# Mixing stage of a hybrid diffusion step: four instead of six output tiles summed during attention, three summed in the end of the stage

## The chip, the core and the metric

The kernel runs on one core of a Trainium2 chip. The metric is device time in microseconds (us) of one execution. The engines are TensorE (PE: matmuls; PEld: its weight loads), VectorE (DVE), ScalarE (ACT), GpSimd (POOL) and SyncE (SP, which issues most DMAs). Each engine works through its own instructions in order; semaphores hold an instruction until what it reads is there.

## The reference

One inference step of a backbone with two layers, 1024 channels, 128 context tokens and 512 latent tokens. Cut to what matters here:

```python
def layer(x, cond, p, lam_init, ropes, ctx):
    h = modulate(rmsnorm(x, p['norm_ffn1']), sh1, sc1)
    x = x + 0.5 * g1 * swiglu(h, p['w_ffn1_in'], p['w_ffn1_out'])
    h = modulate(rmsnorm(x, p['norm_mix']), sh2, sc2)
    y, kv = token_mix(h, p, lam_init, ropes, ctx)
    x = x + g2 * y
    h = modulate(rmsnorm(x, p['norm_ffn2']), sh3, sc3)
    x = x + 0.5 * g3 * swiglu(h, p['w_ffn2_in'], p['w_ffn2_out'])
    return x, kv

def token_mix(h, p, lam_init, ropes, ctx):
    # h @ w_mix_in, split among four head groups of 256 channels each
    ...
    y = jnp.concatenate([y_pool, y_conv, y_gqa, y_diff], axis=-1) @ p['w_mix_out']
    return y, kv_out
```

`y` has 1024 channels: pooling gives the first quarter, a gated convolution the second, grouped-query attention the third, differential attention (with a norm of each head) the last. The change concerns the product with `w_mix_out`.

## The kernel before

Channels lie on the 128 partitions, so x and y are 8 tiles of 128 channels by 640 tokens. All is fp32 by pairs: a number is a high part (`hi`, made by ACT, L174) and a low part (`lo`, made by DVE or POOL, L175), and a product is three matmuls: high by high, high by low, low by high. The tokens go in two halves of 320 columns. One output tile d of the mixing product is thus 8 blocks of y by 3 by 2, 48 matmuls: 36 for y blocks 0 to 5 (`mix_sum`, with 768 columns of weights, `mix_w`) and 12 for blocks 6 and 7 (the "ends"). Blocks 6 and 7 come from differential attention; block 7 is ready last of all, after its head norm (`diff_norm`: head squares on `sel`, a row spread on ACT, transposes on `ident`, a split).

`mix` weaves two generators: `main()` runs the attention (scores, softmax on ACT and DVE, value products), `fill()` gives TensorE other work to do in its waits: projections, the convolution, and at the end the sums of output tiles NO to NO+NE-1, each in two F buffers of PSUM, added to x by three DVE updates (`x_update`, L529). Which comes when is set by two lists of weights, `wm` and `wf`. Tile 0 is opened after that in an S buffer, and gets its 36 matmuls while the last head norm runs.

The end of the stage begins with `mix_ends`, four weight pieces of 512 columns that hold the rows for y blocks 6 and 7 of all tiles (two tiles to a piece). Then a loop goes over the tiles in the ORDER 0, 4, 1, 5, 2, 6, 3, 7. It adds the ends, updates x, and calls `nx.tile(d)`, which prepares the next norm and FFN: squares (ACT L328, summed up on POOL L330), scaling (ACT L434) and, from tile 4 on, sums on DVE (L451 to L457) with splits (L196, L197). The norm's statistics product on `ones` comes once the last tile's square is in the sum. Before the change tile 7 is the one tile whose 36 matmuls come in this loop; its weights are requested when the loop reaches its fifth tile (WLATE = 4).

Weights come through 9 raw buffers, 4 `hi` and 4 `lo` buffers (tags shared by all weights); `mix_w` takes two pieces (512 and 256 columns), with the low part on POOL. PSUM has two S, two F and two H buffers. A scheduler places each instruction on its engine in the order it finds best, not simply as the code is written. In names, S, F and H are PSUM buffers, hi and lo weight pieces, u activation tiles, t scratch, raw weights as loaded, and wa weights of the modulation.

Of the kernel before, what the change touches and what calls it, by code (L numbers as in the profile page):

```python
# [17 lines left out]
WG = 1.7  # L18
LAG = 0.1
LASTN = 384  # L20
NO, NE = 1, 6
WARM = 6
POOLD = ()
SHO = range(8)
SPREAD = 3
RATES = (0.6, 0.42, 0.6)
WLATE = 4
P1A, P0B, P1B = 1, 2, 2
D = 1024
KT = 8  # L30
# [12 lines left out]
ORDER = (0, 4, 1, 5, 2, 6, 3, 7)  # L43
# [39 lines left out]
def hybrid_step(ctx: ExitStack, tc: tile.TileContext, x_in, cc_in, cb_in, w_ada0, w_ada, pv_in, lam_in, w_fin, w_fout, w_min, w_mout,  # L83
# [37 lines left out]
    def PS():  # L121
        return psS.tile([128, 2, 512], F32, tag="S", name=nm("S"))
# [11 lines left out]
    def mm(out, lhsT, rhs, start, stop):  # L134
        PE.matmul(out, lhsT, rhs, start=start, stop=stop)  # L135
# [14 lines left out]
    def raw_tile():  # L150
        return wp.tile([128, 512], F32, tag="raw", name=nm("raw"), bufs=RAWB)
# [31 lines left out]
    def load_w(src, eng=None):  # L183
        return Weights(load_raw(src), eng)
# [312 lines left out]
    def mm3(ps, cuts, w, acts, ks=range(KT), start=True, stop=True):  # L497

        for i, k in enumerate(ks):
            w0, w1 = w.at(k)  # L500
            ah, al = acts[k]
            for p, (w_, a) in enumerate(((w0, ah), (w0, al), (w1, ah))):
                for h in range(2):
                    c0, c1 = cuts[h]
                    mm(ps[h][:, :c1 - c0], w_, a[:, c0:c1],
                       start and i == 0 and p == 0, stop and i == len(ks) - 1 and p == 2)
# [17 lines left out]
    def x_update(d, ps, gate):  # L524

        g = gate[d // 4]
        for c, h, a, b in ((0, 0, 0, NC), (1, 0, NC, HN), (1, 1, 0, HN)):
            xs = x[d][:, h * HN + a:h * HN + b]
            V.scalar_tensor_tensor(out=xs, in0=ps[h][:, a:b], scalar=g[:, d % 4, c:c + 1], in1=xs,  # L529
                                   op0=ALU.mult, op1=ALU.add)  # L530
# [227 lines left out]
    def mix(l, norm, nxt, cache):  # L758
# [524 lines left out]
        def mix_w(d):  # L1283
            return load_w(w_mout[l, d, :, :768], G)

        def mix_sum(w, ps, d, start, stop):

            mm3(ps, CN, w, y, range(6), start, stop)

        def mix_ends():  # L1290

            r = []
            for d0 in (0, 4):
                raws = []
                for d in (d0, d0 + 2):
                    raws.append(raw_tile())
                    nc.sync.dma_start(raws[-1].rearrange("p (d n) -> p d n", d=2), w_mout[l, d:d + 2, :, 768:].rearrange("d p n -> p d n"))
                r.append(Weights(raws))
            return r
# [14 lines left out]
        def drain(*gens):  # L1314
            for g_ in gens:
                next(g_, None)
# [63 lines left out]
            drain(dn)  # L1380
        drain(dn, dn, dn)
        ends = mix_ends()
        for i, d in enumerate(ORDER):
            if d in opened:
                ps = opened[d]
            else:
                p = PS()
                ps = [p[:, 0], p[:, 1]]
            if i == WLATE and NO + NE < KT:
                wl = mix_w(NO + NE)  # L1390
            if d >= NO + NE:
                mix_sum(wl, ps, d, True, False)
            w, k = ends[d // 4], 2 * (d % 4)
            for q in range(2):
                w0, w1 = w.at(k + q)
                ah, al = y[6 + q]
                for p_, (w_, a) in enumerate(((w0, ah), (w0, al), (w1, ah))):
                    for h in range(2):
                        c0, c1 = CN[h]
                        mm(ps[h][:, :HN], w_, a[:, c0:c1], NO <= d < NO + NE and q == 0 and p_ == 0, q == 1 and p_ == 2)  # L1400
            x_update(d, ps, gate)
            nx.tile(d)
# [56 lines left out]
    cache = load_cache(0)  # L1459
    lambdas()  # L1460
    nx = mix(0, nx, lambda: FastNorm(0, 2), cache)
    cache = load_cache(1)
    rows = silu_rows()
# [4 lines left out]
    nx = ffn(1, 0, nx, lambda: Norm(1, 1), pump, RATES[2])  # L1468
    pump.step(1000)
    nx = mix(1, nx, lambda: FastNorm(1, 2), cache)  # L1470
    ffn(1, 2, nx, lambda: None, pump, 0.0)

# [111 lines left out]
```

## Time and profile before

| | us |
|---|---|
| median of 3 runs | 2451.6 (2450.91 to 2452.83) |
| the profiled execution | 2455.93 |
| its span | 2453.9 |
| PE busy in it | 2348.2 |
| DVE busy in it | 2072.6 |

The mean granted clock of TensorE is 0.979 of full speed in it. The span runs from the first instruction to the last; some 2 us of the execution lie around it. A timeline row gives a run of like instructions on one engine: its start, its length, what it is, how many there are, and in brackets how long the engine stood idle before and what released it.

### The profile page before, as it was taken

The page shows a single profiled execution, that of the slowest core. Times are in us where ns is not written, and L with a number is a line of the kernel's source. Part 1 is how long each engine was busy: PE and PEld are TensorE (multiplying, and loading weights), DVE is VectorE, ACT ScalarE, POOL GpSimd, SP SyncE. Part 2 cuts the span into 40 slices and gives each one's busy share as a digit, 9 for nine tenths or more (in the row PEclk, how much of TensorE's full clock was granted, in tenths as well). Part 3 has the DMA queues.
Part 4 walks back from the last instruction along what each step waited for, and adds up shares of the span by engine and source line. Part 5 has one row for each costly group of instructions (what it writes and reads, how often), then busy time and mean ns, then how long its engine had stood idle before and what let it go on. Part 6 is the DMA issues. An engine that isn't in the chain of part 4 may idle for free. (4 is left out here: it accounts for less than half of the span.)

```text
span 2453.9 us, 42559 instructions
## 1 busy us (share of the span) xinstructions
PE 2348.2 (96%) x15497; PEld 2286.1 (93%) x15497; DVE 2072.6 (84%) x3927; ACT 1249.9 (51%) x2498; POOL 377.3 (15%) x424
## 2 busy tenths in 40 slices
PE   7899999999998999999989999999999989999998
PEld 4899999998987999999979999999998979999997
DVE  5999999867878899999989997777687687867876
ACT  3635443557665635434565434445676564434434
POOL 3100000134323101000030100003422330000002
PEclk8999999999999999999989999999999999999999
DMA  7455554423323355555516554323232112223223
GB/s 268 124 181 155 163 165 149 115 89 125 123 80 114 81 182 154 167 156 163 154 61 163 150 163 113 101 76 106 85 141 92 57 40 86 79 83 93 83 71 97
DMA packets 156545, 297.43 MB, mean 121 GB/s; under 512 B 16176, under 2 KB 47536, under 8 KB 156336
## 3 DMA queue, kind: packets, MB, share of 16 engines
q1 hardware_dynamic: 142464, 278.01, 35.4%
q0 software_dynamic: 13872, 16.71, 4.5%
q8 instruction: 122, 2.00, 0.3%
q14 instruction: 87, 0.71, 0.1%
HBM read 263.00 MB, written 14.94 MB: 113 GB/s over the span
## 5 line engine op out<-in xcount | busy, mean ns | idle before, releaser
L174 ACT ACTIVATE hi<-raw 128x512 fp32r<-128x512 f32 (+2 forms) x954 | 574.4, 605 | 879.3 <-PE S L135 385.5
L175 DVE TENSOR_TENSOR lo<-raw,hi 128x512 fp32r<-128x512 f32 (+1 forms) x874 | 571.1, 659 | 109.8 <-ACT hi L174 104.6
L515 PE MATMUL F<-u,hi 128*128 128x322 f32 x2752 | 627.2, 315 | 1.4 <-DVE t L653 0.6
L135 PE MATMUL S<-u,hi 128*128 128x320 f32 (+3 forms) x2144 | 485.9, 317 | 42.1 <-DVE x L529 12.9
L515 PEld LDWEIGHTS F<-u,hi 128*128 128x128 f32 x2752 | 465.0, 190 | 7.2 <-DVE t L653 1.3
L515 PE MATMUL F<-u,lo 128*128 128x322 f32 x1376 | 427.4, 311 | 0.7 <-DVE lo L175 0.7
L135 PE MATMUL S<-u,lo 128*128 128x320 f32 (+3 forms) x1776 | 420.8, 313 | 3.3 <-DVE lo L175 2.5
L135 PEld LDWEIGHTS S<-u,hi 128*128 128x128 f32 x2144 | 361.6, 193 | 54.2 <-issue 16.7
L282 DVE SCALAR_TENSOR_TENSOR wa<-wa,sc 128x1024 bf16<-128x1024 f32 (+1 forms) x264 | 324.3, 1235 | 12.6 <-DMA wa<-in_w_ada_dram 9.0
L135 PE MATMUL S<-e,hi 128*128 128x320 f32 (+2 forms) x1408 | 329.6, 311 | 2.4 <-DVE e L197 1.9
L515 PE MATMUL S<-u,hi 128*128 128x322 f32 x1376 | 313.3, 314 | 12.0 <-DVE t L590 11.0
L135 PEld LDWEIGHTS S<-u,lo 128*128 128x128 f32 x1776 | 306.1, 192 | 4.5 <-DVE lo L175 3.4
L515 PEld LDWEIGHTS F<-u,lo 128*128 128x128 f32 x1376 | 263.9, 192 | 1.0 <-DVE lo L175 1.0
L627 DVE TENSOR_TENSOR raw<-raw,raw 128x512 f32<-128x512 f32 x344 | 238.6, 694 | 8.0 <-DMA raw<-in_w_fin_dram 3.6
L515 PEld LDWEIGHTS S<-u,hi 128*128 128x128 f32 x1376 | 233.0, 190 | 13.0 <-issue 11.2
L135 PEld LDWEIGHTS S<-e,hi 128*128 128x128 f32 x1408 | 237.5, 189 | 5.0 <-DVE e L197 4.8
L135 PE MATMUL F<-u,hi 128*128 128x320 f32 (+1 forms) x1056 | 239.8, 319 | 1.5 <-DVE x L529 0.8
L515 PE MATMUL S<-u,lo 128*128 128x322 f32 x688 | 214.6, 312 | 1.5 <-DVE lo L175 1.5
L572 POOL DMA_DIRECT2D e<-t x51 | 61.5, 1206 | 1003.7 <-DVE t L641 371.7
L540 DVE SCALAR_TENSOR_TENSOR x<-S,gate,x 128x128 f32<-128x128 f32 (+1 forms) x304 | 152.5, 544 | 46.6 <-PE S L135 45.4
L135 PEld LDWEIGHTS F<-u,hi 128*128 128x128 f32 x1056 | 179.0, 193 | 3.9 <-DVE x L529 0.9
L515 PE MATMUL H<-u,hi 128*128 128x322 f32 x688 | 156.3, 313 | 3.0 <-ACT hi L174 3.0
(232 smaller groups left out, 3195.4 us busy)
## 6 DMA issues: line engine op xcount, KB each, us to landing
raw<-in_w_fin_dram SPq DMA_DIRECT2D x352, 256.0 KB
wa<-in_w_ada_dram SPq DMA_DIRECT2D x132, 512.0 KB
raw<-in_w_fout_dram SPq DMA_DIRECT2D x168, 256.0 KB
raw<-in_w_min_dram SPq DMA_DIRECT2D x72, 256.0 KB
e<-t POOLq DMA_DIRECT2D x51, 320.0 KB, 5.3
u<-in_w_ada_dram SPq DMA_DIRECT2D x24, 256.0 KB
KS<-kd SPq DMA_DIRECT2D x16, 384.0 KB
raw<-in_w_mout_dram SPq DMA_DIRECT2D x24, 256.0 KB
```

Source lines behind the costliest of these rows:

```text
L135: PE.matmul(out, lhsT, rhs, start=start, stop=stop)
L174: S.activation(hi[:, :n], src, AF.Copy)
L175: (eng or V).tensor_tensor(out=lo[:, :n], in0=src, in1=hi[:, :n], op=ALU.subtract)
L282: V.scalar_tensor_tensor(out=o, in0=raw, scalar=1.0, in1=rows[i], op0=ALU.mult, op1=ALU.mult, accum_out=m[0][:, b, i:i + 1])
L515: PE.matmul(ps, w_, a, start=start and k == 0 and p == 0, stop=k == 3 and p == 2, skip_group_check=True)
L540: V.scalar_tensor_tensor(out=x[d][:, a:b], in0=w[:, a:b], scalar=g[:, d % 4, c:c + 1], in1=x[d][:, a:b], op0=ALU.mult, op1=ALU.add)
L572: G.dma_start(lo[:, :N].bitcast(F32).rearrange("p (h n) -> p h n", h=2), a, accum_op=ALU.add)
L627: V.tensor_tensor(out=o, in0=a, in1=b, op=ALU.add)
```

## The change

Tiles 1 to 4, not 1 to 6, are summed in `fill()`; the list `wf` is shorter by two entries, so the other fillers spread over attention anew. Tiles 5, 6 and 7 get all their matmuls in the loop at the end. Each one's weights are requested one tile ahead in ORDER, after the sum of the tile before: tile 5's with tile 1, tile 6's with tile 2, tile 7's with tile 3.

```diff
-NO, NE = 1, 6
+NO, NE = 1, 4
-WLATE = 4
...
         ends = mix_ends()
+        late = {}
         for i, d in enumerate(ORDER):
             if d in opened:
                 ps = opened[d]
             else:
                 p = PS()
                 ps = [p[:, 0], p[:, 1]]
-            if i == WLATE and NO + NE < KT:
-                wl = mix_w(NO + NE)
             if d >= NO + NE:
-                mix_sum(wl, ps, d, True, False)
+                mix_sum(late.pop(d), ps, d, True, False)
+            for n in ORDER[i + 1:i + 2]:
+                if n >= NO + NE:
+                    late[n] = mix_w(n)
```

Lines of the changed kernel are one lower (L134 for L135, and so on). Names get new numbers.

PE, layer 0, around the last head norm, before: the head squares (`sel`) follow 18 matmuls after the last value products; F_8662 and F_8715 are filler tiles, S_8823 is tile 0.

```order
L135 MATMUL F_8663<-u_8180,hi_8672 128x320
L135 MATMUL F_8662<-u_8179,lo_8673 128x320
L135 MATMUL F_8663<-u_8179,lo_8673 128x320
L135 MATMUL H_8872<-sel_97,t_8821 128x2 x5
L135 MATMUL F_8715<-u_7477,hi_8721 128x320
...
L135 MATMUL S_8823<-u_8180,hi_8832 128x320 x2
L135 MATMUL S_8823<-u_8179,lo_8833 128x320 x2
L944 MATMUL H_8885<-ident_96,t_8883 128x128 x4
L944 MATMUL H_8891<-ident_96,t_8883 128x128
```

The same place after, where S_8717 is tile 0 and S_8844 tile 4:

```order
L134 MATMUL S_8717<-u_8310,lo_8727 128x320 x2
L134 MATMUL H_8766<-sel_97,t_8715 128x2 x5
L134 MATMUL S_8717<-u_8161,hi_8796 128x320 x2
L134 MATMUL S_8717<-u_8162,hi_8796 128x320 x2
L134 MATMUL S_8717<-u_8161,lo_8797 128x320 x2
L134 MATMUL S_8844<-u_8161,hi_8808 128x320 x2
L134 MATMUL S_8844<-u_8162,hi_8808 128x320 x2
L134 MATMUL S_8844<-u_8161,lo_8809 128x320
L943 MATMUL H_8779<-ident_96,t_8777 128x128 x4
L943 MATMUL H_8785<-ident_96,t_8777 128x128
```

Where 108 matmuls lay between `sel` and the transposes (`ident`), 11 do now; the 108 lie ahead of `sel`, after the last value products. Ahead of those, 54 fewer stand in each layer.

PE, layer 0, tile 5 in the end loop, after; S_8901 is tile 1, S_8937 tile 5, S_9024 tile 2. Before, tile 5 had only 12 matmuls there.

```order
L134 MATMUL S_8901<-u_8788,lo_8797 128x320 x2
L134 MATMUL S_8937<-u_7553,hi_8906 128x320 x2
...
L134 MATMUL S_8937<-u_8401,lo_8907 128x320 x2
L134 MATMUL S_9024<-u_8161,hi_8800 128x320 x2
L134 MATMUL S_9024<-u_8162,hi_8800 128x320
L134 MATMUL S_8937<-u_7763,hi_8910 128x320 x2
```

Tile 5's first piece (hi_8906) serves 24 matmuls, its second (hi_8910) 12, and three of tile 2's come between them.

ACT, layer 0, the same place, after; u are splits of tiles 0 and 4 for the next FFN, x_82 is tile 1.

```order
L195 ACTIVATE u_8879<-t_8863 128x322
L173 ACTIVATE hi_8906<-raw_8902 128x512
L195 ACTIVATE u_8884<-t_8875 128x322
L195 ACTIVATE u_8887<-t_8874 128x322
L195 ACTIVATE u_8891<-t_8874 128x322
L327 ACTIVATE t_8929<-x_82 128x640
L433 ACTIVATE t_8932<-x_82,scl_8834 128x128
L173 ACTIVATE hi_8910<-raw_8904 128x256
```

Tile 5's two pieces stand between the splits of the next FFN; before, the one late tile's two pieces stood next to each other.

## Rows read from the trace of the kernel before

**Rows 1.** Page, part 1: busy us, share of the span, instructions.

```profile
PE 2348.2 (96%) x15497; PEld 2286.1 (93%) x15497; DVE 2072.6 (84%) x3927; ACT 1249.9 (51%) x2498; POOL 377.3 (15%) x424
```

**Rows 2.** Windows: us, busy time (count) by engine, PEclk, DMA share, GB/s.

```profile
560.00:747.00 187.00, 178.92 (x1227) 171.21 (x1226) 146.96 (x312) 126.45 (x294) 59.62 (x66) 0.98 0.33 111
773.00:805.00 32.00, 23.04 (x119) 22.13 (x119) 29.46 (x62) 21.64 (x53) 14.34 (x13) 0.79 0.12 40
1757.00:1944.00 187.00, 178.75 (x1225) 170.24 (x1225) 147.53 (x311) 128.29 (x293) 59.91 (x70) 0.98 0.30 101
1968.00:1997.00 29.00, 19.92 (x120) 18.99 (x121) 26.44 (x57) 21.59 (x53) 13.65 (x12) 0.94 0.06 19
```

**Rows 3.** Timeline of PE, layer 0: start, us, engine, line, operation, idle before.

```profile
746.08 0.76 PE L135 MATMUL H<-p,u 128*128 128x256 f32 x5
...
749.32 1.17 PE L135 MATMUL H<-sel,t 128*128 128x2 f32 x10
...
768.11 0.71 PE L944 MATMUL H<-ident,t 128*128 128x128 f32 x5
...
775.16 0.82 PE L135 MATMUL S<-u,hi 128*128 128x320 f32 x4 [0.92 <-DVE x L529]
...
794.69 1.40 PE L135 MATMUL S<-u,hi 128*128 128x320 f32 x4 [2.73 <-ACT t L434]
...
810.95 2.17 PE L135 MATMUL H<-ones,t 128*128 128x1 f32 x10 [2.29 <-POOL t L330]
```

**Rows 4.** Timeline of PE, layer 1.

```profile
1943.71 0.76 PE L135 MATMUL H<-p,u 128*128 128x256 f32 x5
...
1963.95 0.71 PE L944 MATMUL H<-ident,t 128*128 128x128 f32 x5
...
1983.27 1.27 PE L135 MATMUL S<-u,hi 128*128 128x320 f32 x4
1984.34 0.74 PE L135 MATMUL S<-u,lo 128*128 128x320 f32 x2
...
1995.65 0.74 PE L135 MATMUL S<-u,hi 128*128 128x320 f32 x4
1996.24 0.45 PE L135 MATMUL S<-u,lo 128*128 128x320 f32 x2
...
2001.65 1.67 PE L135 MATMUL H<-ones,t 128*128 128x1 f32 x10 [0.72 <-POOL t L330]
```

**Rows 5.** Timeline of DVE, layer 0.

```profile
771.94 0.81 DVE L197 TENSOR_TENSOR u<-u,u 128x640 fp32r<-128x640 f32 x1
...
773.89 2.16 DVE L529 SCALAR_TENSOR_TENSOR x<-S,mod,x 128x128 f32<-128x128 f32 x6
775.98 1.21 DVE L282 SCALAR_TENSOR_TENSOR wa<-wa,sc 128x1024 f32<-128x1024 f32 x1
```

**Rows 6.** Timeline of DVE, layer 1.

```profile
1966.98 0.83 DVE L197 TENSOR_TENSOR u<-u,u 128x640 fp32r<-128x640 f32 x1 [0.80 <-ACT u L196]
...
1975.16 2.52 DVE L197 TENSOR_TENSOR u<-t,u 128x322 fp32r<-128x322 f32 x2
...
1978.67 2.10 DVE L197 TENSOR_TENSOR u<-t,u 128x322 fp32r<-128x322 f32 x5
```

**Rows 7.** Timeline of ACT, layer 0.

```profile
752.78 0.74 ACT L936 ACTIVATE t<-s 128x640 f32<-128x640 f32 x1 [0.46 <-POOL s L1253]
...
779.24 0.92 ACT L174 ACTIVATE hi<-raw 128x512 fp32r<-128x512 f32 x2
```

**Rows 8.** Groups by line and shape, POOL: busy, mean ns, idle before, releasers.

```profile
L175 POOL TENSOR_TENSOR lo<-raw,hi 128x512 fp32r<-128x512 f32 x64 | 86.4, 1355 | 230.4 <-ACT hi L174 224.9 <-PE S L135 4.9 <-DVE t L789 0.3
...
L175 POOL TENSOR_TENSOR lo<-raw,hi 128x256 fp32r<-128x256 f32 x16 | 13.7, 853 | 5.1 <-ACT hi L174 4.8 <-PE S L135 0.2
```

**Rows 9.** Timeline of POOL, both layers.

```profile
777.59 1.81 POOL L330 TENSOR_TENSOR t<-t,t 128x640 f32<-128x640 f32 x1 [18.41 <-ACT t L328]
...
1974.79 2.54 POOL L175 TENSOR_TENSOR lo<-raw,hi 128x512 fp32r<-128x512 f32 x2 [0.76 <-ACT hi L174]
```

## The prediction

> **What bounds the kernel now.** I read the page's busy shares first. TensorE's matmuls (PE) are busy 96% of the span and VectorE (DVE) 84% [rows 1]. The change leaves every matmul in the program and only moves some, so it can pay only where PE stands still. I therefore cut the mixing stage of each layer by the table of windows [rows 2] and then read the timelines at the cuts. The reader is to see two places of opposite kind. During attention PE is busy 178.9 of 187 us at a clock of 0.98 while DVE is busy 147: softmax work has nearly enough matmuls under it. At the end of the stage PE is busy only 23 of 32 us in layer 0 at a clock of 0.79, and DVE 29.5 of 32; in layer 1 it is 19.9 and 26.4 of 29 us. There DVE is what the end waits for, and PE has room. The change carries matmuls from the first place to the second.
>
> Three marks per layer divide the time. P is the end of the last value products (128x256): 746.84 and 1944.47 [rows 3, 4]. T is the end of the split of y block 7, from which the last two y blocks can be used: 772.75 and 1967.81 [rows 5, 6]. S is the start of the statistics product of the next norm (on `ones`), which needs the last tile's sum: 810.95 and 2001.65. Before, P to T is 25.9 and 23.3 us, T to S is 38.2 and 33.8.
>
> **Attention, up to P.** In the new PE order 54 matmuls of 320 columns fewer stand ahead of P in each layer. At the full clock (2.4 GHz) one takes (1996.24 - 1995.65)/4 = 0.147 us [rows 4]: 7.9 us. What they covered, softmax's waits, does not go with them. Now 8.1 of 187 us are idle; with about 4% fewer filler matmuls I add an estimated 1.5 us. Bounds: 0 (the cover was spare) and 7.9 (each was cover). I take the low side, since the remaining filler still fills 96% of the window. Term: -6.4 us per layer.
>
> **From P to T.** Before, 18 matmuls come before the head-square products (on `sel`) and 108 between these and the transposes; after, 108 and 11. So PE no longer covers the chain from the squares over DVE, POOL and the ACT spread to the transposes. That chain takes 753.52 - 749.32 = 4.2 us in layer 0 [rows 3, 7], and 11 matmuls are 1.6 of it. From the transposes to T it is 4.6 and 3.9 us, as before [rows 3 to 6]. After: 108 x 0.147 = 15.9, plus 4.2, plus 4.6 or 3.9, is 24.7 and 24.0. Term: -1.2 in layer 0, +0.6 in layer 1.
>
> **From T to S.** Here 61 matmuls more wait: most of tiles 5, 6 and 7. Step by step from T, with layer 0's durations:
> PE restarts when the first update has freed an S buffer, at +2.4 (775.16) [rows 3]. Tile 1's 12 matmuls: +4.2. Tile 5's first weight piece needs a buffer which tile 1's weights hold until then, and on ACT it stands behind the splits of tile 4; ACT reached the weight piece at this place at 779.24, which is +6.5, and needs 0.46 [rows 7]: +7.0. POOL forms the low half in 1.36 [rows 8] and with the hand-overs I set +8.5. Four of the 24 matmuls run meanwhile; 20 are left, 2.9 us at the full clock. At the low level (1.2 GHz) one takes (1984.34 - 1983.27)/4 = 0.267 [rows 4], so 5.3: +11.4 or +13.8. The second piece finds no other free buffer than the first one's: 0.46, then 0.85 on POOL [rows 8] and 0.2 of hand-overs: +12.9 or +15.3. Another 20 matmuls (8 of the piece, 12 of the ends): +15.8 or +18.2. The three updates are half of 2.16 [rows 5], so tile 6 starts at +17.0 or +19.4. From here weights are ready, their buffers being free during the tile before: 48 matmuls of tile 6 take 7.1, 12 of tile 3 1.8, 48 of tile 7 7.1: +33.0 or +35.4. Then the update 1.1, the ACT square (as wide as the spread of 0.74 [rows 7]) and the POOL sum 1.8 [rows 9]: S at +36.6 or +39.0. Against 38.2 that is -1.6 to +0.8, against 33.8 it is +2.8 to +5.2; the middles are -0.4 and +4.0.
>
> Two weight pairs more per layer now have their low halves formed by POOL while DVE is the busy engine. In layer 1 a pair ran on POOL at 1974.79 for 2.54 [rows 9], and two DVE splits that began at 1975.16 took 2.52, where five took 2.10 shortly after [rows 6]: 1.26 each instead of 0.42. The rows alone bound the loss by the time of two pairs, 0 to 5.1 us per layer (2 x 2.54); DVE stands on the path of the end only in the updates, so I take about a quarter, +1.1. Term with it: +0.7 in layer 0, +5.1 in layer 1. The Trainium skill (SBUF — State Buffer, Who interferes with whom) says that a DVE instruction with two SBUF inputs contends with a GpSimd instruction that reads SBUF, and that whichever is first keeps the shared ports while the other stands still; the two splits above agree with it. Taken at its word for both pairs, and with DVE the pace of the end throughout, it would add 2 x 4.0 us to the sum, 2452.0 on the median.
>
> The waiting instructions hold others. On ACT the splits and scalings of tiles 4 and 1 stand around the late pieces; on POOL a square sum stands behind tile 5's low half; on DVE weight preparation for the next FFN (raw buffers) stands ahead of tile 5's update, and in layer 0 eight instead of three products of 1.21 us on `wa` [rows 5]: 6.1 us, hidden only while PE is the slower. I cost the requests themselves at nothing: the queue carries the same bytes and DMA is busy 0.12 and 0.06 in the two ends [rows 2]. If a request came late, tile 5 would wait for it.
>
> **Sum.** Layer 0: -6.4 - 1.2 + 0.7 = -6.9. Layer 1: -6.4 + 0.6 + 5.1 = -0.7. Together -7.6 us, or 2455.9 to 2448.3 of the profiled execution. That execution is 4.3 us above the median, 2451.6; on the median the same difference gives 2444.0.
>
> **Rivals.**
> *The low clock slows the late sums (slower).* In layer 0's end the granted clock is 0.79; after an idle of 2.73 us four matmuls take 1.40 where four at the full clock take 0.74 [rows 2 to 4]. Now PE waits several times in a row there (before the transposes, after T, for tile 5's two pieces), and 108 matmuls of late sums follow. If all run at 0.267 instead of 0.147 it costs 13.0 us per layer; 2.4 are in the middle above, so +10.6 per layer and +21 in both: 2465. The sum's gain is used up by 63 such matmuls beyond the 20 per layer already counted. Against it: layer 1's end has 0.94 now, and PE would be busier there than it is now. On gaps of this sort the Trainium skill (TensorE: Matmul & The Clock Gate, HAM oscillation) warns that they make the array run slow again for work that follows; by it the time is this rival's.
> *DVE still bounds the end.* With DVE at 29.5 of 32 us, the late sums may simply fill PE's gaps, and T to S stays as it is: -6.4 - 1.2 and -6.4 + 0.6, together -13.4, or 2438.2. Against it: tile 5's two pieces follow each other on a path that has no slack.
> *Attention isn't paced by PE.* If softmax's chain sets the pace, the 54 matmuls bring nothing up to P: -7.6 + 12.8 = +5.2, or 2456.8. Against it: PE is busy 96% there and at the full clock.
> *Part of it.* Half the attention term only (+6.4), or two POOL pairs that hold DVE for their whole 5.1 us in each layer (+8.0): 2450 to 2452. For it: the splits at 1975.16 [rows 6, 9]; against it: DVE has other idle gaps to lose first, 2.5 us in each end [rows 2].
>
> **How the numbers follow.** About 0.2%, 4.9 us, is what a measurement of this kernel can tell: faster is below 2446.7, slower above 2456.5. I give the sum 0.45 (0.38 faster, 0.07 within), DVE-bound end 0.13 (faster), partial 0.20 (0.17 within, 0.03 slower), low clock 0.12 (slower), attention not paced 0.10 (half within, half slower). Faster 0.51, same 0.29, slower 0.20. The sum's own range is 2439 to 2449, from both clock levels and part of the port loss; with the others on either side I set 2436 to 2457.
>
> **What would show it.** P comes 6 to 8 us earlier after the start of attention in both layers. The `sel` products follow some 100 matmuls after P, and PE then idles about 2.5 us before the transposes; T is 24 to 25 us after P. PE waits for an ACT weight piece and a POOL low half before tile 5, twice; T to S is 37 to 40 us in both layers. I am wrong if P does not move, if T to S passes 45 us, or if it stays at 38 and 34 or less.

## The result and the profile after

The changed kernel is slower: 2488.68 us median (2488.06 to 2490.18) against 2452.22 us for the kernel before beside it, ratio 1.0143 with a 95% interval of 1.0131 to 1.0155. The forecast was 2444.0 with a range of 2436 to 2457; it had the sign wrong.

The profiled execution after has a span of 2486.0 us, 32.1 more than before. The three marks of the prediction divide it, with the first softmax exponential of each attention as a fourth (in layer 0 the mark lies 0.7 us ahead of it, in every run alike; columns: layer 0, layer 1; us):

| stretch | before | after | forecast of the change | measured |
|---|---|---|---|---|
| first exponential to P | 185.7, 183.2 | 193.2, 187.3 | -6.4, -6.4 | +7.6, +4.1 |
| P to T | 25.9, 23.3 | 24.9, 24.2 | -1.2, +0.6 | -1.0, +0.8 |
| T to S | 38.2, 33.8 | 50.8, 44.0 | +0.7, +5.1 | +12.6, +10.1 |

These add up to +34.2; the stretches outside give back 2.1. Windows of the changed kernel, the columns as in [rows 2]; the first and third run from 16 us before the first exponential to P, the second and fourth from T to S:

```profile
545.00:754.30 209.30, 188.06 (x1252) 178.11 (x1251) 162.21 (x330) 131.75 (x307) 67.17 (x76) 0.95 0.31 103
...
779.20:830.00 50.80, 38.35 (x213) 35.50 (x212) 48.71 (x85) 28.95 (x66) 24.44 (x19) 0.89 0.25 78
1761.70:1965.20 203.50, 182.33 (x1238) 172.92 (x1237) 156.31 (x327) 130.81 (x303) 64.97 (x73) 0.97 0.28 96
...
1989.40:2033.30 43.90, 35.81 (x212) 33.44 (x210) 34.50 (x66) 28.30 (x66) 20.74 (x19) 0.93 0.10 31
```

In attention PE is idle 21.2 of 209.3 us where 10.4 of 201.7 were idle before, and 21.2 of 203.5 where it was 10.6 of 199.2: with less to do it waits longer. In the end of layer 0 DVE is busy 48.7 of 50.8 us, for the kernel before 29.5 of 32 [rows 2], or 34.2 of the whole 38.2. The matmuls that came into the end filled little of PE's idle time there: it is idle 12.4 us of T to S where it was 11.5, in layer 1 8.1 where it was 10.2.

The timeline of PE in layer 0, which answers to [rows 3]:

```profile
752.99 1.34 PE L134 MATMUL H<-p,u 128*128 128x256 f32 x10
...
770.07 1.17 PE L134 MATMUL H<-sel,t 128*128 128x2 f32 x10
...
775.66 0.76 PE L943 MATMUL H<-ident,t 128*128 128x128 f32 x5 [2.69 <-ACT t L935]
...
782.04 1.41 PE L134 MATMUL S<-u,hi 128*128 128x320 f32 x4 [0.25 <-DVE x L528]
...
786.78 1.30 PE L134 MATMUL S<-u,hi 128*128 128x320 f32 x4 [2.05 <-ACT hi L173]
...
795.61 0.56 PE L134 MATMUL S<-u,lo 128*128 128x320 f32 x2 [1.91 <-POOL lo L174]
...
801.36 0.82 PE L134 MATMUL S<-u,hi 128*128 128x320 f32 x4 [1.22 <-DVE x L528]
...
814.41 1.40 PE L134 MATMUL S<-u,hi 128*128 128x320 f32 x4 [4.01 <-DVE x L528]
...
830.04 1.28 PE L134 MATMUL H<-ones,t 128*128 128x1 f32 x10 [2.30 <-POOL t L329]
```

From P (754.33) on, the `sel` products, the 2.7 us of uncovered chain and T (779.24) lie as the prediction has them; P itself is 7.5 us later than before, where 6.4 us earlier was forecast. From T the steps are: tile 5 starts at +7.5, its second low half is there at +16.4, tile 6 starts at +22.1, tile 7 at +35.2, S at +50.8. The last two rows with DVE as releaser, PE's waits of 1.22 and 4.01 us, are where the time goes. DVE's own timeline at T, at these places and at the last update, and POOL's below it:

```profile
778.42 0.82 DVE L196 TENSOR_TENSOR u<-u,u 128x640 fp32r<-128x640 f32 x1
...
797.84 2.31 DVE L281 SCALAR_TENSOR_TENSOR wa<-wa,sc 128x1024 bf16<-128x1024 f32 x1
...
800.09 2.17 DVE L528 SCALAR_TENSOR_TENSOR x<-S,mod,x 128x128 f32<-128x128 f32 x6
...
805.86 2.31 DVE L281 SCALAR_TENSOR_TENSOR wa<-wa,sc 128x1024 bf16<-128x1024 f32 x1
...
813.14 1.12 DVE L528 SCALAR_TENSOR_TENSOR x<-S,mod,x 128x128 f32<-128x128 f32 x3
...
825.46 1.12 DVE L528 SCALAR_TENSOR_TENSOR x<-S,mod,x 128x128 f32<-128x128 f32 x3
```

```profile
797.55 3.19 POOL L174 TENSOR_TENSOR lo<-raw,hi 128x512 fp32r<-128x512 f32 x2 [2.00 <-ACT hi L173]
...
805.64 3.13 POOL L174 TENSOR_TENSOR lo<-raw,hi 128x512 fp32r<-128x512 f32 x2 [2.01 <-ACT hi L173]
```

A product on `wa` takes 1.21 us [rows 5] and 2.31 beside a POOL pair, and the pair 3.1 to 3.2 instead of some 2.2 (1.36 and 0.85 [rows 8]). PE runs out of work at 810.4; the update that it then waits for stands on DVE behind products on `wa`, sums and splits, and starts at 813.14.

In attention the largest new wait is in layer 1. PE, and then DVE, at one place:

```profile
1873.09 1.30 PE L943 MATMUL H<-ident,t 128*128 128x128 f32 x5 [5.54 <-DVE vc L196]
```

```profile
1859.53 1.34 DVE L196 TENSOR_TENSOR t<-t,t 128x640 fp32r<-128x640 f32 x1
...
1872.12 0.49 DVE L788 TENSOR_TENSOR t<-F,R 128x320 f32<-128x320 f32 x1 [5.71 <-DMA qd<-t]
1872.53 0.41 DVE L196 TENSOR_TENSOR u<-H,u 128x256 fp32r<-128x256 f32 x1
1872.86 0.21 DVE L196 TENSOR_TENSOR vc<-H,vc 128x64 fp32r<-128x64 f32 x1
```

The reader is to follow it backwards. PE's transposes wait for an H buffer, which the splits of v (vc) free. These stand on DVE behind the scaling of a filler's projection, and that waits for one of the five scratch buffers `t`, out of which the filler for the second differential pair copies its q to memory; the first row is DVE's writing of it. No such wait is in the trace of before.

### The profile page after: what moved, and what is told of

It is laid out like the page before. It is cut to its first block, busy times and chain, and to the rows that moved or that the text cites. A ratio compares the mean times of both kernels' runs of the same rounds, so it can differ in the third digit from the quotient of the medians.

```text
span 2486.0 us, 42554 instructions
## 1 busy us (share of the span) xinstructions
PE 2356.4 (95%) x15497; PEld 2290.6 (92%) x15497; DVE 2077.9 (84%) x3915; ACT 1249.1 (50%) x2498; POOL 371.7 (15%) x424
## 3 DMA queue, kind: packets, MB, share of 16 engines
q1 hardware_dynamic: 142464, 278.01, 34.9%
## 5 line engine op out<-in xcount | busy, mean ns | idle before, releaser
L134 PE MATMUL S<-u,hi 128*128 128x320 f32 (+3 forms) x2240 | 505.0, 318 | 36.3 <-DVE x L539 7.8
L514 PEld LDWEIGHTS F<-u,hi 128*128 128x128 f32 x2752 | 464.8, 190 | 8.8 <-DVE u L196 2.7
L134 PE MATMUL S<-u,lo 128*128 128x320 f32 (+3 forms) x1824 | 433.7, 314 | 6.0 <-POOL lo L174 3.4
L134 PEld LDWEIGHTS S<-u,hi 128*128 128x128 f32 x2240 | 378.0, 193 | 48.0 <-ACT hi L173 11.8
L134 PE MATMUL S<-e,hi 128*128 128x320 f32 (+2 forms) x1408 | 330.3, 312 | 2.2 <-DVE e L196 2.0
L281 DVE SCALAR_TENSOR_TENSOR wa<-wa,sc 128x1024 f32<-128x1024 f32 (+1 forms) x264 | 323.4, 1232 | 9.3 <-DMA wa<-in_w_ada_dram 6.3
L514 PE MATMUL S<-u,hi 128*128 128x322 f32 x1376 | 313.8, 314 | 13.0 <-DVE t L589 10.5
L134 PEld LDWEIGHTS S<-u,lo 128*128 128x128 f32 x1824 | 315.0, 192 | 8.3 <-POOL lo L174 4.9
L514 PEld LDWEIGHTS S<-u,hi 128*128 128x128 f32 x1376 | 232.9, 190 | 14.4 <-issue 10.7
L134 PEld LDWEIGHTS S<-e,hi 128*128 128x128 f32 x1408 | 237.9, 189 | 4.8 <-DVE e L196 4.5
L134 PE MATMUL F<-u,hi 128*128 128x320 f32 (+1 forms) x960 | 222.8, 320 | 0.9 <-DVE u L196 0.6
L134 PEld LDWEIGHTS F<-u,hi 128*128 128x128 f32 x960 | 164.5, 195 | 2.6 <-DVE u L196 1.1
```

Of the source, the lines that this page charges most:

```text
L281: V.scalar_tensor_tensor(out=o, in0=raw, scalar=1.0, in1=rows[i], op0=ALU.mult, op1=ALU.mult, accum_out=m[0][:, b, i:i + 1])
L514: PE.matmul(ps, w_, a, start=start and k == 0 and p == 0, stop=k == 3 and p == 2, skip_group_check=True)
```

## The experiments

Times of the stretches are from each kernel's profile (layer 0, layer 1).

**Places or cover?** Fewer fillers also mean a shorter list of shares, so every projection and convolution step moves to a later part of attention. The first run takes the kernel before with all its six sums, and moves only the places:

```diff
-        wf = ([3.3] * 6 + [0.1]) * 2 + [3.3] * 12 + [4.9] * NE
+        wf = ([3.3] * 6 + [0.1]) * 2 + [3.3] * 12 + [4.9 * 4 / 6] * NE
```

> The kernel before with its six sums (tiles 1 to 6) packed into the share of the attention that the changed kernel gives to its four, so that the projections and convolution steps stand over the attention as in the changed kernel, with no matmul taken away. Spacing theory (the change hurt attention because these steps moved against the softmax units): the stretch from the first softmax exponential to the last value product (185.7 and 183.2 us before, 193.2 and 187.3 after) is again 193 us or more in layer 0 and 187 or more in layer 1, PE idle in it and the 16 us ahead of it some 20 us instead of 10.5; the whole is about 2460 to 2475. Cover theory (it hurt because 72 matmuls of cover per layer were taken away): the stretch stays at 186 and 183 us with 10 us idle, and the whole within 5 us of 2452.

2485.38 us, ratio 1.0131 (1.0108 to 1.0153): as slow as the changed kernel, and slower than this text expected. Attention took 198.2 and 189.7 us. The windows, from 16 us before the first exponential to P, and DVE's waits for a DMA in layer 1's (us in total, times, longest):

```profile
545.10:759.40 214.30, 191.62 (x1288) 181.94 (x1287) 163.66 (x333) 133.08 (x309) 69.43 (x78) 0.96 0.30 102
1761.70:1967.50 205.80, 186.86 (x1273) 177.64 (x1272) 157.53 (x330) 131.86 (x305) 66.76 (x75) 0.98 0.28 96
```

```profile
DVE t L789 <- DMA qd<-t: 5.9, 1, 5.9
```

PE is idle 22.7 and 18.9 us with all six sums in the list, and the same wait for the scratch is there. P to T is 32.0 and 26.1 us, T to S 37.4 and 35.9. Moving the places does it. (18 of the matmuls that stood ahead of P before fall behind it here too, 2.6 us at 0.147.) The reverse run takes the changed kernel and leaves the places as they were:

```diff
-        wf = ([3.3] * 6 + [0.1]) * 2 + [3.3] * 12 + [4.9] * NE
+        wf = ([3.3] * 6 + [0.1]) * 2 + [3.3] * 12 + [4.9] * 6
```

> The changed kernel with two empty entries at the end of the list of filler weights, so that projections, convolution and the four sums stand over the attention where they stood before, and only the places of the last two sums are empty. Spacing theory: the stretch from the first exponential to the last value product falls from 193.2 and 187.3 back to 186 and 183 us or some us below, with about 10 us idle of PE; the end of the stage stays long, so the whole comes to 2470 to 2478. Cover theory: the stretch stays at 190 us or more, with idle time of PE where the two sums were, and the whole stays within 5 us of 2488.

2461.04 us, ratio 1.0025 (1.0015 to 1.0034): some 28 of the 35 us are gone, and it is below the window expected. Attention is 184.5 and 183.2 us with 10.5 and 10.7 idle:

```profile
546.50:747.00 200.50, 189.99 (x1305) 181.71 (x1304) 160.02 (x333) 133.12 (x309) 69.05 (x78) 0.98 0.34 111
1746.20:1945.40 199.20, 188.55 (x1291) 179.71 (x1289) 159.19 (x330) 132.53 (x305) 66.28 (x75) 0.98 0.29 99
```

The two empty places do not lie in attention. Matmuls of the filler sums (F buffers) between P and the transposes, layer 0, before, in the changed kernel and here (us, PE busy, PEclk, DMA share, GB/s):

```profile
746.84:768.10 21.26, 13.72 (x90) 1.00 0.54 179
754.33:775.60 21.27, 10.78 (x72) 1.00 0.60 192
747.04:759.40 12.36, 2.65 (x18) 1.00 0.58 187
```

In the kernel before, 90 stood behind P: tiles 5 and 6, the two that the change takes away, and half of tile 4. So the 54 matmuls fewer ahead of P in the changed kernel are not the sums taken away. They are tile 3 and the other half of tile 4, which the shorter list pushed behind P. With the places held, as many stand ahead of P as before (the windows show 53 more in each layer than in the changed kernel), and P to T is 16.0 and 15.7 us, 8 to 9 us less than in the changed kernel. What stays is the end, T to S 50.9 and 44.5 us.

**What made the end grow?** First the low halves of the weights of tiles 5, 6 and 7 are not formed, and the high halves stand in their place, so the outputs differ and the number of matmuls does not:

```diff
-            return load_w(w_mout[l, d, :, :768], G)
+            return load_w(w_mout[l, d, :, :768], G if d < NO + NE else "hi")
...
+            if eng == "hi":
+                return hi, hi
             (eng or V).tensor_tensor(out=lo[:, :n], in0=src, in1=hi[:, :n], op=ALU.subtract)
```

> The changed kernel, but the low halves of the weights of tiles 5, 6 and 7 are not formed: their high halves are used in place of them, so the outputs differ; the number of matmuls stays. Port theory (the end of the stage grew from 38.2 to 50.8 and from 33.8 to 44.0 us mainly because POOL's three low-half pairs stop DVE and hold up tile 5): the end falls by 6 us or more per layer, the whole to 2476 or less. Order theory (it grew because 61 matmuls more and DVE's sums, weight preparation and updates now wait for each other in a row): the end falls by 3 us or less per layer, the whole stays above 2482.

2479.45 us, ratio 1.0103 (1.0077 to 1.0129), between the two expectations. T to S is 44.7 and 41.1: the POOL pairs, and PE's waits for them, cost 6.2 and 2.8 us of the 12.6 and 10.1. Second, with the old places, the late weights are not requested one tile ahead but go early into the two key buffers, which attention needs no more:

```diff
+        def mix_early(d):
+            k = sp.tile([128, 1536], F32R, tag="KS", name=nm("KS"), bufs=2)
+            w = Weights([])
+            for r, c in zip(load_raw(w_mout[l, d, :, :768]), (0, 512)):
+                n = r.shape[-1]
+                hi, lo = k[:, c:c + n], k[:, 768 + c:768 + c + n]
+                S.activation(hi, r, AF.Copy)
+                G.tensor_tensor(out=lo, in0=r, in1=hi, op=ALU.subtract)
+                w.parts.append((hi, lo))
+            return w
...
+        late = {d: mix_early(d) for d in (5, 6)}
         drain(dn, dn, dn)
...
+            if d == 5:
+                late[7] = mix_early(7)
```

> The changed kernel with the two empty filler entries (2461 us), and the late weights not in the four hi and lo buffers but in the two key buffers, which attention no longer needs then: tiles 5 and 6 are split before the last head norm ends, tile 7 after tile 5's sum. Weights theory (the end grew from 38.2 to 50.9 and 33.8 to 44.5 us by waiting for late pieces and by POOL stopping DVE): the end falls to 42 us or less in layer 0 and 37 or less in layer 1, the whole to 2448 or less, below the kernel before. Work theory (it grew because 61 matmuls, 9 us, were put on a row of steps in which DVE's sums and updates set the pace and PE's gaps are too early or too late to take them): the end stays above 46 and 41 us, the whole above 2455.

2456.16 us, ratio 1.0009 (1.0000 to 1.0019): neither expectation on the whole. T to S, in windows of this kernel:

```profile
764.80:804.60 39.80, 35.13 (x217) 33.61 (x216) 35.22 (x69) 26.43 (x62) 18.29 (x15) 0.93 0.18 55
1958.50:1998.70 40.20, 34.44 (x213) 33.31 (x211) 34.32 (x67) 26.54 (x62) 16.86 (x15) 0.92 0.06 19
```

In layer 0, 50.9 falls to 39.8, which the weights theory has at 42 or less. In layer 1, 44.5 falls to 40.2 and not to 37; PE and DVE are now about equally busy, and the 72 matmuls that more than before stand behind T, 10.6 us at 0.147, still cost 6.4. P to S is 56.0 and 56.4 us against 64.1 and 57.2 before. Yet the whole is not faster. From S in layer 0 to the first exponential of layer 1 it takes 953.3 us, in the kernel before 950.4, and 947.9 (changed kernel) or 948.3 (the run with the old places) with the long end.

The key buffers were not free in layer 0: `ada_fetch` gives the same two (tag `KS`) to the weights `wa`. SP's requests for `wa` around P in the kernel before, and then here, where the first of this mixing stage comes only at 787.08:

```profile
735.84 0.34 SPq L266 DMA_DIRECT2D wa<-in_w_ada_dram  x1
...
757.69 0.38 SPq L266 DMA_DIRECT2D wa<-in_w_ada_dram  x1
```

```profile
787.08 14.02 SPq L265 DMA_DIRECT2D wa<-in_w_ada_dram  x3
```

So the edit did two things in layer 0. From T to S, DVE had 7 products on `wa` (9.6 us) in the run with the old places and has 2 (2.4 us) here; how much of the 11.1 us is theirs, no run shows. Layer 1, which has none there, shows the early weights alone: 4.3 of the 10.6 us by which its end had grown in the run with the old places. And what is not done comes later. From S to layer 1's first exponential DVE is busy 861.0 us here, 852.8 before and 845.6 in the changed kernel; between P and the last update of layer 0 the products on `wa` number 2, 11 and 16, the instructions on the next FFN's weights 11, 9 and 9. That this makes the 3 to 5 us is argued from these counts; no run gave the early weights buffers of their own.

**The other way and halfway.** The kernel before with seven sums, none late:

```diff
-NO, NE = 1, 6
+NO, NE = 1, 7
```

> The kernel before with seven sums in the fillers (tile 7 as well), none in the end of the stage: the change taken one step the other way. If the end is a row of waits in which each late sum costs its matmuls and more (late sums of 72 matmuls added 10 to 12.6 us), leaving out the 36 of tile 7 shortens the end by 5 us or more per layer, and 36 more fillers add 5.3 us or less to the attention: the whole within 5 us of 2452 or a few us below. If attention suffers from any other spacing of the fillers, its stretch grows by 5 us or more per layer and the whole is above 2460.

2471.03 us, ratio 1.0071 (1.0050 to 1.0091), above 2460 as the second expectation has it. Attention grew by 6.8 us in both layers, with 32 matmuls more ahead of P (4.7 us at 0.147) and all places moved the other way; the run does not part the two. T to S is 35.0 and 34.5:

```profile
783.10:818.00 34.90, 20.94 (x104) 18.59 (x105) 33.20 (x71) 25.52 (x61) 15.07 (x13) 0.82 0.10 31
1982.20:2016.70 34.50, 21.07 (x106) 18.14 (x106) 32.12 (x68) 25.55 (x61) 14.84 (x13) 0.81 0.00 1
```

With no late sum at all the end is not 5 us shorter, but 3.2 us in layer 0 and 0.7 longer in layer 1. DVE is busy 33.2 of 34.9 and 32.1 of 34.5 us, so its work is nearly the whole end. That fits the reading of the profile that DVE bounds the end before. The kernel before, its own six sums, with tile 7's weights prepared early by the `mix_early` above:

```diff
+        late = {d: mix_early(d) for d in (7,)}
...
-            if i == WLATE and NO + NE < KT:
-                wl = mix_w(NO + NE)
```

> The kernel before (six sums in attention), with tile 7's weights split early into a key buffer in place of the late pieces in hi and lo buffers. Weights theory: the waits for its pieces leave the end, which falls by 2 us or more per layer; the whole 2446 to 2450. Work theory: the end stays as it is, 38 and 34 us, since tile 7 is the last tile and its sum is reached when DVE gets there; the whole within 3 us of 2452.

2457.92 us, ratio 1.0017 (1.0007 to 1.0026); T to S 36.0 and 35.8. Neither theory holds: the end is 2.2 us shorter in layer 0 and 2.0 longer in layer 1, and the whole is not shorter. Two late tiles, both early, with one empty place (against the run with early weights):

```diff
-NO, NE = 1, 4
+NO, NE = 1, 5
...
-        late = {d: mix_early(d) for d in (5, 6)}
+        late = {d: mix_early(d) for d in (6, 7)}
...
-            if d == 5:
-                late[7] = mix_early(7)
```

> Between the kernel before and the changed one: five sums in attention (tiles 1 to 5), one empty entry behind them so that all steps keep their old places, tiles 6 and 7 late with both weights split early into the two key buffers. With four sums and early weights the stretch from the last value product to the statistics product fell from 64.1 and 57.2 to 56.0 and 56.4 us, with TensorE the bound in its second part and 6 us of uncovered chain in its first. If the balance is the point, five sums cover more of that chain and leave DVE and PE even in the end: 54 to 56 us, attention within 1.5 us of 185.7 and 183.2, the whole 2446 to 2453. If DVE or the chain of the last tile sets the end whatever the number of late sums, the stretch is 58 us or more and the whole within 4 us of 2454.

2463.54 us, ratio 1.0034 (1.0024 to 1.0044): P to S 60.1 and 59.0, as the second expectation has it, but the whole slower than it. Attention is 185.3 and 186.8 us. Here it takes 955.4 us from S of layer 0 to the first exponential of layer 1, with one product on `wa` between P and the last update.

**The scratch.** In the changed kernel, only these two tiles move out of `t`:

```diff
-            qh, ql = T(F32R), T(F32R)
+            qh, ql = (U(), U()) if j else (T(F32R), T(F32R))
             split(qh[:, :N], ql[:, :N], t[:, :N])
```

> The changed kernel; only the two scratch tiles of the second differential pair's q, from which a DMA copies to memory, are taken from the activation buffers (33 of them) and not from the five t buffers. In the changed kernel DVE stood 2.3 us in layer 0 and 8.2 us in layer 1 before a projection's scaling, because that DMA still held the t buffer it was to write; in the kernel before it never did. Scratch theory: these waits vanish, PE's waits of 2.1 and 5.5 us on DVE behind them too, and attention falls from 193.2 and 187.3 us by 2 to 4 and 5 to 8 us, the whole to 2475 to 2482. Rival (these waits cover others: the moved steps' DVE and ACT work collides with the softmax units anyway): the idle time of PE turns up elsewhere in the attention, and the whole stays within 4 us of 2488.

2476.27 us, ratio 1.0095 (1.0079 to 1.0111), the window expected. Attention is 187.9 and 178.1 us, 5.3 and 9.2 less than after, and DVE has no wait for a DMA in it.

```profile
545.00:749.20 204.20, 185.87 (x1254) 174.60 (x1253) 161.68 (x331) 131.76 (x307) 67.35 (x76) 0.97 0.32 106
1757.20:1951.40 194.20, 180.15 (x1238) 170.03 (x1236) 157.35 (x327) 131.03 (x303) 65.35 (x73) 0.99 0.30 101
```

In layer 1 that is 5.1 us less than before the change, near the -6.4 forecast. In layer 0 it is still 2.2 more, with 18.3 us idle in many small gaps, the largest 2.7 us. Does the edit do something by itself? The same two lines in the kernel before:

> The kernel before with the one edit of the scratch run (the second pair's q scratch from the activation buffers). In the kernel before no instruction waited for that scratch, so if the edit cured the changed kernel by removing a wait and by nothing else, it does nothing here: attention 185.7 and 183.2 us to within 1.5, the whole within 4 us of the kernel before. If the edit is worth something by itself (another order, fewer t buffers in use), attention is 3 us or more shorter here too.

2452.61 us, ratio 0.9993 (0.9983 to 1.0003), attention 186.0 and 181.9, within the 1.5 us expected. It does nothing there that is clear of noise, so in the changed kernel it cured a wait. Both cures with the changed kernel's own places (against the run with early weights):

```diff
-            qh, ql = T(F32R), T(F32R)
+            qh, ql = (U(), U()) if j else (T(F32R), T(F32R))
...
-        wf = ([3.3] * 6 + [0.1]) * 2 + [3.3] * 12 + [4.9] * 6
+        wf = ([3.3] * 6 + [0.1]) * 2 + [3.3] * 12 + [4.9] * NE
```

> The changed kernel with its own spacing (four filler entries) and both cures: the second pair's q scratch from the activation buffers, and the late weights split early into the key buffers. If the 35 us of loss were these two things and the remaining collisions of layer 0, they add up: attention 187.9 and 178.1 us as with the scratch alone, the end some 40 us in both layers, the whole 2455 to 2462. If the two share a cause, or the early split falls on a busy attention, the whole stays above 2466.

2467.68 us, ratio 1.0055 (1.0037 to 1.0072), just above the bound of 2466. Attention is 186.8 and 181.0, T to S 39.7 and 39.3; in layer 1 DVE waits 1.5 us for the same kind of scratch of the first pair, which was left in `t`, and ACT 1.6 us for the load of early weights. From S of layer 0 to layer 1's first exponential it takes 953.7 us, with 2 products on `wa` as above. The cures act, but do not add up to the kernel before, and no run beat that clear of noise.

## Why the prediction was wrong

*Attention, up to P* is the step that failed: "-6.4 us per layer" was +7.6 and +4.1, 24.5 us of the error. The step took fewer matmuls to be all that changed before P, and those to be carried from attention to the end. But the two sums taken away stood behind P already, and the list of filler shares is one scale for all fillers: with two entries fewer, tile 3 and half of tile 4 fell behind P, and projections, splits, copies and scalings of the differential heads moved against the softmax units. One run moved the places with no sum taken away and lost 31 us; one kept the places and lost 6. The fillers are not matmuls alone: they take DVE, POOL, H buffers and scratch. In layer 1 the largest part is the scratch that a DMA still held; without that wait the term is -5.1. Layer 0's remainder is many small gaps, which no run took apart.

The bound of 7.9 for lost cover was thus not a bound: it counted what missing cover could uncover, not what a step does at another place. None of the rivals had this cause. The one nearest in time, the low clock, had 2465. "Attention isn't paced by PE" (2456.8) is answered by the scratch run, where layer 1's attention with 54 matmuls fewer is 5.1 us shorter.

*From P to T* was right to 0.2 us in each layer, with the 2.7 and 2.0 us of PE waiting before the transposes.

*From T to S* had the right order of steps and the wrong durations from tile 5's second piece on. Tile 6 starts at +22.1 and +20.1 where +17.0 to +19.4 was worked out, and tile 7 at +35.2 and +28.9 where its start would be +25.9 to +28.3. From T on 72 matmuls more wait, not 61: 16 of the ends had run by T in either kernel. What was missing is DVE's queue. I had counted eight products on `wa` in layer 0 in place of three, 6.1 us more, and called them hidden only while PE is the slower; they weren't, since updates stand behind them in order. In layer 1, without such products, early weights took 4.3 us off the end; 6.4 of its growth stayed, with PE and DVE both busy 34 of 40 us. In both layers the last update came 3 to 4 us behind tile 7's matmuls, not 1.1, and S 3.5 us behind that, not 2.5. For the port loss I took a quarter of 5.1, +1.1; leaving the low halves out (of three pairs, where the bound counted two) saved 6.2 and 2.8, with tile 5's waits for them among it. The Trainium skill's rule (SBUF — State Buffer, Who interferes with whom) counted for more in layer 0 than I let it, and the trace agrees with it: a product on `wa` took 2.31 us beside a pair, 1.21 else. Matmuls at the low clock, the rival I named for a slower kernel, were not it: from T to S the granted clock rose from 0.82 to 0.89 in layer 0 and fell from 0.95 to 0.93 in layer 1. PE's busy time grew there by 11.7 and 12.2 us for 73 matmuls more, 10.7 at the full clock, so the clock cost an estimated 0.9 and 1.5 us, not 10.6. (That price was itself mis-summed: the middle of the step holds 1.2 us of low clock, not 2.4, so the rival would be 11.8 per layer.)

## What to carry to other kernels

Where a list of shares or weights sets the places of interleaved work, taking an entry out moves all the others: compare the places first, and test the move with the work held. A filler step costs every resource that it touches, and a scratch buffer out of which a DMA copies is one; look for what is held longest when such a step comes later. A buffer that one stage needs no more may be another's: before lending it, look up who else shares it. On an engine that works in order and is busy nearly all of a stretch (DVE here 48.7 of 50.8 us), do not call anything in its queue hidden: count what stands ahead of each instruction that another engine waits for.

## What the hardware showed that was not expected

POOL and DVE slow each other, and both pay: beside a POOL pair a DVE product on `wa` took 2.31 us in place of 1.21, and the pair 3.13 to 3.19 in place of 2.2. It is not the low halves alone: a DVE sum of 0.48 us took 1.86 beside a POOL square sum (791.98 in the changed kernel). The scratch was held long: in the changed kernel's layer 1 the q tile was written on DVE by 1860.9, and DVE got the buffer at 1872.1.

And one profile says less than it seems to: the profiled executions of the kernel with early weights and of that with both cures were short (2451.98 and 2463.75 us against medians of 2456.16 and 2467.68), so stretches of one profile don't sum to a difference of medians to better than some 5 us.
